# Seven-product units in attention's V, V ahead of Q in one head group, block moves over two queues

## The chip, the cores and the metric

The kernel runs on one core of one Trainium2 chip. The core's engines work side by side, each through its own queue in order: PE (TensorE: matmuls, with a weight load, PEld, ahead of each), DVE (VectorE), ACT (ScalarE), POOL (GpSimd) and SP (SyncE, here used only to start DMAs). DMAs are started by the queue of an engine and run beside the engines. The metric is the device time of one execution in microseconds, as a median over runs: 2028.35 us before (three runs, 2028.28 to 2033.81).

## The reference, cut to what matters

A decoder trunk of two layers on 256 tokens of 2048 channels. Layer 0 has a pooling mixer, layer 1 attention; each is followed by a gated feed-forward part and has two layer norms. The change is in layer 1's attention. Three dilated branches share q, k and v and are merged by their softmax denominators, which is one softmax over all keys, weighted by how many branches see a key:

```python
for i in range(DEPTH):                       # i = 1 is the attention layer
    ...
    k_shared = (h @ shared_w_k).reshape(B_, S, N_HEADS, HEAD_DIM)   # 16 heads of 128
    v_shared = (h @ shared_w_v).reshape(B_, S, N_HEADS, HEAD_DIM)
    mix = dilated_attention(h, k_shared, v_shared, attn_w_q[j], attn_w_o[j])
    h = layer_norm(DEEPNORM_ALPHA * h + mix, ln1_g[i], ln1_b[i])
...
def dilated_attention(h, k, v, w_q, w_o):
    q = (h @ w_q).reshape(B_, S, N_HEADS, HEAD_DIM)
    for window, dil in ((128, 1), (512, 4), (2048, 16)):
        o, lse = _dilated_branch(q, k, v, window, dil)
        ...
    o = jnp.sum(softmax(lses)[..., None] * outs, axis=0)
    return o.reshape(B_, S, D_MODEL) @ w_o
```

All is float32.

## The kernel before, in words

**Units.** Every weight matrix is read in blocks of 512 rows by 512 columns, one load of 1024 KB each on SP's queue. The list `units` holds one entry per block, in the order of the program; `run_units` walks it. For unit i it first calls `ahead(i)`: that issues the loads up to unit i+5 (three buffers `raw`) and the splits up to unit i+3 (four pairs of buffers `wh`, `wl`). A split makes two halves of a weight block whose sum is the weight: ACT casts the high half (L82), DVE subtracts it from the weight to get the low half (L83). x has been split in the same way. A product of float32 numbers is then two or three matmuls: high by high, low by high, high by low. After that come the matmuls of unit i. A function given to `later(n, fn)` runs after n further units; PE, DVE, ACT and SP get its instructions in their queues at that place.

**Three kinds of unit.** `group` (L165, L166) makes q, k and the output projection with the channels in the partitions: 16 matmuls of 512 columns and 16 of 256. `group_tm` (L238 to L240) makes v with the tokens in the partitions: 24 matmuls of 512 columns. The third kind, "seven products", is a form of a 2x2 block product (tokens in two halves, the block's columns in two halves, its rows in two halves) that takes seven block products instead of eight, at the price of sums of weights and sums of x. It is used in the feed-forward part before, not in attention. Its unit comes as two entries of the list with one load: part a (three products, 18 matmuls of 256 columns) and part b (four, 24 matmuls), L227 to L229. `split_sums` makes their weights: for a, two casts of ACT (L103), and on DVE a subtract (L104), two low halves (L106), two more subtracts (L107, L109); for b two casts (L96) and two low halves (L97). The seven leaves its results in four PSUM banks (`t0`, `t1`, `s2`, `s3`), and the function `early` has to add the last two banks in, five times a quarter.

**Attention.** Four head groups of four heads (hq 0 to 3). Before, each has four units of K, four of Q and four of V; sixteen units of the output projection follow. After the last unit of Q `qk_post` sets the rest: `scores` for heads 0 and 1, and one unit later for heads 2 and 3 (PE L988, L989, then a softmax, mostly on DVE, L994 to L1011); `blocks` turns the probabilities of two heads: a DVE transpose of 32x32 blocks (L1034) into the buffer `pb`, and then 16 DMAs that put the blocks in their places (L1043), of 32 partitions by six pieces of 32 numbers each, eight after one unit and eight after two, all on SP's queue. The buffer `pb` comes from the pool `hp` with five buffers, four of which hold the stream of layer 1, so one is free: the next block transpose waits until the DMAs of the one before have landed. `outputs` multiplies v by the turned probabilities (PE L1056, L1057) and splits the result (ACT, DVE L1059). For the last head group PE turns the probabilities itself (`transposes`, L1026), since there is little work between its softmax and the use.

Of the kernel before, what the change touches and what calls it, by code (L numbers as in the profile page):

```python
# [32 lines left out]
def trunk(ctx: ExitStack, tc: tile.TileContext, x, pool_w_in, pool_w_grp, pool_scale, pool_w_out,  # L33
# [14 lines left out]
    def bank(nm):  # L48
        return psp.tile([P, 512], F32, name=nm, tag="ps")
# [70 lines left out]
    def later(n, fn):  # L120
        if n == 0:
            fn()
        else:
            pending.append([n, fn])
# [157 lines left out]
    def quad_tile(nm):  # L282
        return xcp.tile([P, 4, 2, XW], F32R, name=nm, tag="xc")
# [659 lines left out]
    scale = 1.0 / math.sqrt(P)  # L943
    qk, pr, oq, pT, vts = {}, {}, {}, {}, {}

    def v_post(c):
        def post(t, ps):
            if t == 0:
                vts[c] = pools["attn"].tile([P, 2, 512], F32, name="vt", tag="vt")
                A.copy(vts[c][:, 0, :], ps)  # L950
            else:
                V.tensor_copy(vts[c][:, 1, :], ps)
                if c == 3:
                    later(1, lambda: transposes(c, (0, 1)))
                    later(2, lambda: transposes(c, (2, 3)))
                later(2 if c == 3 else 4, lambda: outputs(c, (0, 1)))
                later(3 if c == 3 else 7, lambda: outputs(c, (2, 3)))
        return post

    def qk_post(nm, hq):  # L960
        def post(ps):
            later(2 if hq == 0 and nm == "k" else 0, lambda: evac(ps))

        def evac(ps):
            ap = pools["attn"]
            o = ap.tile([P, 4, T], F32, name=nm, tag=nm)
            qk[nm] = o

            if hq == 0 and nm == "k":
                norm_evac(ps, 4, lambda m: o[:, m, :])  # L970
            else:
                for m in range(4):
                    A.copy(o[:, m, :], ps[m][:, T:])
                    V.tensor_tensor(o[:, m, :], o[:, m, :], ps[m][:, :T], OP.add)
            if nm == "q":
                later(2, lambda: scores(hq, range(0, 2)))
                later(3, lambda: scores(hq, range(2, 4)))
                if hq < 3:
                    later(4, lambda: blocks(hq, (0, 1)))
                    later(7, lambda: blocks(hq, (2, 3)))  # L980
        return post

    def scores(hq, ms):
        ap = pools["attn"]
        for m in ms:
            ps = bank("s")
            q, k = qk["q"][:, m, :], qk["k"][:, m, :]
            PE.matmul(ps[:, 0:P], q[:, :P], k[:, :P], start=True, stop=True)  # L988
# [24 lines left out]
    def turned(hq, ms):  # L1013
        pool, tag = (pools["attn"], "pT") if ms[0] == 0 else (lnp, "sq")
        t = pool.tile([P, 2, 3 * P], F32, name="pTs", tag=tag)
        for m in ms:
            pT[hq, m] = t[:, m % 2]
        return t

    def transposes(hq, ms):  # L1020
        t = turned(hq, ms)
        for m in ms:
            ps = bank("pT")
            s = pr.pop((hq, m))[0]
            for i in range(3):
                PE.transpose(ps[:, i * P:(i + 1) * P], s[:, i, :], ident)  # L1026
            A.copy(t[:, m % 2], ps[:, :3 * P])


    def blocks(hq, ms):  # L1030
        two = pr.pop((hq, ms[0]))[2]
        pr.pop((hq, ms[1]))
        b = hp.tile([P, 6 * P], F32, name="pb", tag="h")
        V.transpose(b, two.rearrange("p h s k -> p (h s k)"))  # L1034

        t = turned(hq, ms)
        to = t.rearrange("p h s -> p (h s)").rearrange("p (k a j) -> p a k j", k=6, a=4)
        fr = b.rearrange("p (k b j) -> p b k j", k=6, b=4)

        def move(rows):  # L1040
            for i in rows:
                for j in range(4):
                    nc.sync.dma_start(to[32 * j:32 * j + 32, i], fr[32 * i:32 * i + 32, j])  # L1043

        later(1, lambda: move((0, 1)))
        later(2, lambda: move((2, 3)))

    def outputs(hq, ms):
        if ms[0] == 0:
            oq[hq] = quad_tile("o")  # L1050
        vt = vts[hq]
        for m in ms:
            hd = slice(m * P, (m + 1) * P)
            ps = bank("o")
            t = pT.pop((hq, m))
# [12 lines left out]
    ffn(1)  # L1068
# [141 lines left out]
```

## Time and profile before

| | |
|---|---|
| median of three runs | 2028.35 us |
| profiled execution's own time | 2030.49 us |
| span of the profile | 2028.6 us |
| last matmuls of V: first, second, last head group | about 1000, 1073 and 1218 us of the span |
| granted PE clock over the span | full |

A row of instructions reads: start, duration, engine, line, operation, tiles out<-in, shapes, count; a bracket holds the idle time before it and what ended it. A row of the table of stretches gives, for each engine, busy time and (x) number of instructions, then the granted clock and the DMA share. A row of a wait reads: engine and operation that waits <- who ends it: total us, count, longest. "SPq" is SP's queue issuing DMAs. A row of issues gives the shortest/median/longest time (ns) of the issuing instruction, and a second line the time from issue to landing (us).

### The profile page before, as it was taken

The page shows a single profiled execution, that of the slowest core. Times are in us where ns is not written, and L with a number is a line of the kernel's source. Part 1 is how long each engine was busy: PE and PEld are TensorE (multiplying, and loading weights), DVE is VectorE, ACT ScalarE, POOL GpSimd, SP SyncE. Part 2 cuts the span into 40 slices and gives each one's busy share as a digit, 9 for nine tenths or more (in the row PEclk, how much of TensorE's full clock was granted, in tenths as well). Part 3 has the DMA queues.
Part 4 walks back from the last instruction along what each step waited for, and adds up shares of the span by engine and source line. Part 5 has one row for each costly group of instructions (what it writes and reads, how often), then busy time and mean ns, then how long its engine had stood idle before and what let it go on. Part 6 is the DMA issues. An engine that isn't in the chain of part 4 may idle for free.

```text
span 2028.6 us, 31127 instructions
## 1 busy us (share of the span) xinstructions
PE 2021.7 (100%) x12496; PEld 1809.4 (89%) x12496; DVE 1674.5 (83%) x1998; ACT 1257.2 (62%) x1685; POOL 75.0 (4%) x111
## 2 busy tenths in 40 slices
PE   9999999999999999999999999999999999999999
PEld 8898988899889988889888888998899989989987
DVE  6859887899789999879756657787889888989898
ACT  5544686667766676657533444577667676667672
POOL 2000000000000001100000000000000000100100
PEclk9999999999999999999999999999999999999999
DMA  8565467666655757864566554557666756666665
GB/s 257 201 206 188 165 209 210 190 192 225 210 191 187 234 188 219 232 226 165 191 197 195 169 185 168 187 178 216 187 198 197 228 187 213 198 213 196 209 214 180
DMA packets 278305, 405.92 MB, mean 200 GB/s; under 512 B 80414, under 2 KB 95668, under 8 KB 277904
## 3 DMA queue, kind: packets, MB, share of 16 engines
q1 hardware_dynamic: 266144, 389.72, 57.9%
q0 software_dynamic: 11584, 13.55, 4.4%
q8 instruction: 98, 1.61, 0.3%
q10 hardware_dynamic: 432, 0.66, 0.1%
q14 instruction: 47, 0.39, 0.1%
HBM read 380.01 MB, written 2.10 MB: 188 GB/s over the span
## 4 chain that ended last, share of the span: by engine, by line
PE 99%; DMA 0%; SPq 0%; DVE 0%; ACT 0%; issue 0%; DVEq 0%
PE acc L165 43%; PE acc L166 22%; PE t L238 3%; PE t L239 3%; PE t L240 3%; PE acc L169 3%; PE acc L170 3%; PE acc L168 3%; PE s L228 3%; PE s L229 3%; PE s L227 3%; PE t L228 2%; PE t L227 2%; PE t L229 2%; PE s L989 0%; PE o L1056 0%
## 5 line engine op out<-in xcount | busy, mean ns | idle before, releaser
L165 PE MATMUL acc<-xc,wh 128*128 128x512 f32 x3264 | 1151.9, 396 | 0.0
L166 PE MATMUL acc<-xc,wl 128*128 128x256 f32 x3264 | 916.3, 281 | 0.0
L83 DVE TENSOR_TENSOR wl<-raw,wh 128x2048 fp32r<-128x2048 f32 (+2 forms) x320 | 692.4, 2168 | 248.4 <-ACT wh L82 243.9
L165 PEld LDWEIGHTS acc<-xc,wh 128*128 128x128 f32 x3264 | 616.0, 189 | 143.7 <-DVE o L1059 0.6
L82 ACT CAST wh<-raw 128x2048 fp32r<-128x2048 f32 (+2 forms) x320 | 578.1, 1812 | 225.7 <-PE acc L165 118.3
L166 PEld LDWEIGHTS acc<-xc,wl 128*128 128x128 f32 x3264 | 615.5, 189 | 0.5
L96 ACT CAST wh<-raw 128x1024 fp32r<-128x1024 f32 x112 | 117.4, 1053 | 150.2 <-DVE raw L107 134.1
L97 DVE TENSOR_TENSOR wl<-raw,wh 128x1024 fp32r<-128x1024 f32 x112 | 133.8, 1221 | 0.5 <-ACT wh L96 0.5
L103 ACT CAST wh<-raw 128x1024 fp32r<-128x1024 f32 x112 | 87.7, 832 | 41.2 <-PE acc L165 24.7
L106 DVE TENSOR_TENSOR wl<-raw,wh 128x1024 fp32r<-128x1024 f32 x112 | 101.9, 951 | 1.3 <-ACT wh L103 0.9
L586 ACT ACTIVATE c<-u,cv 128x256 f32<-128x256 f32 x172 | 89.5, 593 | 19.4 <-DVE f L649 8.2
L228 PE MATMUL t<-wl,g 128*128 128x256 f32 x328 | 92.2, 281 | 0.0
L227 PE MATMUL t<-wh,g 128*128 128x256 f32 x328 | 92.1, 281 | 0.0
L229 PE MATMUL t<-wh,g 128*128 128x256 f32 x328 | 91.9, 280 | 0.0
L271 POOL DMA_DIRECT2D ht<-w x24 | 20.3, 847 | 1808.1 <-ACT wh L103 1060.1
L577 ACT COPY u<-acc 128x256 f32<-128x256 f32 x164 | 54.0, 372 | 46.9 <-PE acc L166 46.8
L229 PE MATMUL s<-wh,xs 128*128 128x256 f32 x296 | 82.6, 279 | 0.0
L228 PE MATMUL s<-wl,xs 128*128 128x256 f32 x296 | 82.6, 279 | 0.0
L227 PE MATMUL s<-wh,xs 128*128 128x256 f32 x296 | 82.5, 279 | 0.0
L591 ACT ACTIVATE a<-u,cv 128x256 f32<-128x256 f32 x172 | 73.6, 500 | 12.3 <-DVE g L659 6.5
L591 ACT ACTIVATE u<-u,cv 128x256 f32<-128x256 f32 x172 | 73.5, 500 | 0.0
L109 DVE TENSOR_TENSOR raw<-raw 128x1024 f32<-128x1024 f32 x56 | 68.6, 1225 | 1.9
(279 smaller groups left out, 3444.8 us busy)
## 6 DMA issues: line engine op xcount, KB each, us to landing
raw<-in_ffn_w_up_dram SPq DMA_DIRECT2D x160, 1024.0 KB, 4.9
raw<-in_ffn_w_down_dram SPq DMA_DIRECT2D x80, 1024.0 KB, 5.1
raw<-in_pool_w_out_dram SPq DMA_DIRECT2D x16, 1024.0 KB, 5.0
raw<-in_shared_w_k_dram SPq DMA_DIRECT2D x16, 1024.0 KB, 5.1
raw<-in_attn_w_q_dram SPq DMA_DIRECT2D x16, 1024.0 KB, 5.3
raw<-in_shared_w_v_dram SPq DMA_DIRECT2D x16, 1024.0 KB, 5.9
raw<-in_attn_w_o_dram SPq DMA_DIRECT2D x16, 1024.0 KB, 5.0
raw<-in_pool_w_in_dram SPq DMA_DIRECT2D x12, 1024.0 KB, 5.6
```

The source lines that it names most:

```text
L82: A.copy(wh[i][:, s], r[:, s])
L83: V.tensor_tensor(wl[i][:, s], r[:, s], wh[i][:, s].bitcast(F32), OP.subtract)
L96: A.copy(h[:, :, n], r[:, :, n])
L97: V.tensor_tensor(l[:, :, n], r[:, :, n], h[:, :, n].bitcast(F32), OP.subtract)
L106: V.tensor_tensor(l[:, k, n], r[:, k, n], h[:, k, n].bitcast(F32), OP.subtract)
L165: PE.matmul(ps[m], h[:, k, c], q[:, k, :, :T], start=st, stop=False)
L166: PE.matmul(ps[m][:, :T], l[:, k, c], q[:, k, 0, :T], start=False, stop=sp and not shifted)
L227: PE.matmul(to, xh, h[:, k, n], start=opens and kk == 0, stop=False)
L228: PE.matmul(to, xh, l[:, k, n], start=False, stop=False)
L229: PE.matmul(to, xl, h[:, k, n], start=False, stop=ends and kk == 1)
L586: A.activation(c[:, m, :], u[:, m, 2:], AF.Identity, scale=cv[:, 2, j:j + 1], bias=cv[:, 3, j:j + 1])
L591: A.activation(to[:, m, :], u[:, m, i:i + T], AF.Copy, scale=cv[:, i, j:j + 1])
```

## The change

In the second, third and fourth head group some of the four V units become sevens: three in the second group (its units 1, 2, 3), three in the third, one in the fourth (unit 3). The sums of x that they need are formed once, in `v_sums`, on DVE and ACT, for the three quarters of x used, one after another at the end of the units that follow the first group's Q; a seven's v is added together by `v_early` and `v_post`. In the second head group V stands between K and Q. The block moves of a batch are issued together, eight on SP's queue and eight on POOL's. The last head group uses block transposes and moves too, and PE's transposes are gone. The distances in units after Q at which scores, block transposes and outputs come are written out for each group.

```diff
     def v_post(c):
         def post(t, ps):
-            if t == 0:
-                vts[c] = pools["attn"].tile([P, 2, 512], F32, name="vt", tag="vt")
-                A.copy(vts[c][:, 0, :], ps)
+            v = v_tile(c)[t]
+            if c > 0:
+                V.tensor_tensor(v, v, ps, OP.add)
+            elif t == 0:
+                A.copy(v, ps)
             else:
-                V.tensor_copy(vts[c][:, 1, :], ps)
-                if c == 3:
-                    later(1, lambda: transposes(c, (0, 1)))
-                    later(2, lambda: transposes(c, (2, 3)))
-                later(2 if c == 3 else 4, lambda: outputs(c, (0, 1)))
-                later(3 if c == 3 else 7, lambda: outputs(c, (2, 3)))
+                V.tensor_copy(v, ps)
         return post
 
+    def v_early(c):
+        def early(p16, p75):
+            v0, v1 = v_tile(c)
+            left, right = v0[:, :256], v0[:, 256:]
+            A.copy(left, p16[:, :256])
+            V.tensor_tensor(right, left, p16[:, 256:], OP.add)
+            V.tensor_tensor(v1[:, :256], right, p75[:, :256], OP.add)
+            V.tensor_tensor(right, right, p75[:, 256:], OP.add)
+            V.tensor_tensor(v1[:, 256:], v1[:, :256], p75[:, 256:], OP.add)
+        return early
+
+    vsums = {}
+
+    def v_sums(q, then):
+        ap = pools["attn"]
+        x = H[q]
+        a11, a12, a21, a22 = (x[:, k:k + 2, t * P:t * P + P] for k, t in ((0, 0), (2, 0), (0, 1), (2, 1)))
+        f = ap.tile([P, 4, T], F32, name="f", tag="k")
+        d = [f[:, i].rearrange("p (k t) -> p k t", k=2) for i in range(4)]
+        V.tensor_tensor(d[0], a21, a22, OP.add)
+        V.tensor_tensor(d[1], d[0], a11, OP.subtract)
+        V.tensor_tensor(d[2], a21, a11, OP.subtract)
+        V.tensor_tensor(d[3], a12, d[1], OP.subtract)
+
+        def rest():
+            if q < 3:
+                t = quad_tile("xsum")
+                vsums[q] = [[t[:, i, hl, :T].rearrange("p (k t) -> p k t", k=2) for hl in range(2)] for i in range(4)]
+                split_act(t, f)
+                then()
+                return
...
+        later(1, rest)
...
             if nm == "q":
-                later(2, lambda: scores(hq, range(0, 2)))
-                later(3, lambda: scores(hq, range(2, 4)))
-                if hq < 3:
-                    later(4, lambda: blocks(hq, (0, 1)))
-                    later(7, lambda: blocks(hq, (2, 3)))
+                s0, b0, b1, o0, o1 = ((2, 4, 7, 8, 11), (2, 4, 7, 12, 14), (9, 11, 14, 15, 18), (2, 3, 5, 7, 8))[hq]
+                later(s0, lambda: scores(hq, range(0, 2)))
+                later(b0, lambda: blocks(hq, (0, 1)))
+                later(s0 + 1, lambda: scores(hq, range(2, 4)))
+                later(b1, lambda: blocks(hq, (2, 3)))
+                later(o0, lambda: outputs(hq, (0, 1)))
+                later(o1, lambda: outputs(hq, (2, 3)))
+                if hq == 0:
+                    later(4, lambda: v_sums(3, lambda: v_sums(1, lambda: v_sums(2, lambda: None))))
         return post
...
-        def move(rows):
-            for i in rows:
+        def move():
+            for i in range(4):
                 for j in range(4):
-                    nc.sync.dma_start(to[32 * j:32 * j + 32, i], fr[32 * i:32 * i + 32, j])
-
-        later(1, lambda: move((0, 1)))
-        later(2, lambda: move((2, 3)))
+                    by = nc.sync if i < 2 else nc.gpsimd
+                    by.dma_start(to[32 * j:32 * j + 32, i], fr[32 * i:32 * i + 32, j])
+
+        later(1, move)
...
+    def v_group(hq):
+        js = (0, 1, 2, 3)
+        seven = {0: (), 1: (1, 2, 3), 2: (1, 2, 3), 3: (3,)}[hq]
+        group_tm(shared_w_v, rows4, 512 * hq, 512, xsrcs, v_post(hq),
+                 seven={j: (lambda j=j: vsums[j]) for j in js if j in seven}, early=v_early(hq))
+
     for hq in range(4):
         x0 = hq == 0
         group(shared_w_k, rows4, 512 * hq, 512, psrcs if x0 else xsrcs, qk_post("k", hq), mode="x" if x0 else "ab")
+        if hq == 1:
+            v_group(hq)
         group(attn_w_q[0], rows4, 512 * hq, 512, xsrcs, qk_post("q", hq))
-        group_tm(shared_w_v, rows4, 512 * hq, 512, xsrcs, v_post(hq))
+        if hq != 1:
+            v_group(hq)
```

PE's queue after the second head group's K, where the first group's first two outputs are made, reads as follows before the change (`wh210` is the high half of the 211th unit's weights, `xc` the split x, `acc` a bank of q).

```order
L1056 MATMUL o_9938<-pTs_9758,vt_9759 128x256
L1057 MATMUL o_9938<-pTs_9758,vt_9759 128x128
L1056 MATMUL o_9943<-pTs_9758,vt_9759 128x256
L1057 MATMUL o_9943<-pTs_9758,vt_9759 128x128
L165 MATMUL acc_9971<-xc_9247,wh210_9814 128x512
L166 MATMUL acc_9971<-xc_9247,wl210_9815 128x256
```

After the change, at the end of the first V unit, which follows the same outputs, and the start of the first seven (`t0`, `t1`, `s2` are banks of v):

```order
L238 MATMUL t1_10023<-wh210_9844,xc_9247 128x512
L239 MATMUL t1_10023<-wl210_9845,xc_9247 128x512
L240 MATMUL t1_10023<-wh210_9844,xc_9247 128x512
L227 MATMUL s2_10024<-wh211_9890,xc_9310 128x256
L228 MATMUL s2_10024<-wl211_9891,xc_9310 128x256
L229 MATMUL s2_10024<-wh211_9890,xc_9310 128x256
```

V's plain unit and its sevens have come to where Q's first unit stood.

SP's queue around the first of the second head group's two batches before (`raw` is a buffer of a weight block, the number behind x counts the DMAs of a row):

```order
L72 DMA raw_10302<-in_attn_w_q_dram 128x4x512
L72 DMA raw_10338<-in_attn_w_q_dram 128x4x512
L1043 DMA pTs<-pb 32x6x32 x8
L72 DMA raw_10388<-in_attn_w_q_dram 128x4x512
L1043 DMA pTs<-pb 32x6x32 x8
L72 DMA raw_10434<-in_attn_w_q_dram 128x4x512
```

The moves of both of the second head group's batches stand on SP after the change like this:

```order
L72 DMA raw_10582<-in_shared_w_v_dram 128x4x512
L72 DMA raw_10632<-in_shared_w_v_dram 128x4x512
L1081 DMA pTs<-pb 32x6x32 x8
L72 DMA raw_10726<-in_shared_w_v_dram 128x4x512
L1081 DMA pTs<-pb 32x6x32 x8
L72 DMA raw_10835<-in_shared_w_v_dram 128x4x512
```

A batch now has one row of eight on SP instead of two, with a load between them; the other eight stand on POOL's queue, 64 in all, one row behind another.

DVE's queue at the end of the last head group after the change (`pb` the turned blocks, `vt` v, `wl250` the low half of an output projection's unit):

```order
L1062 TENSOR_SCALAR p_11659<-p_11659,mx_11671 128x256
L83 TENSOR_TENSOR wl250_11690<-raw250_11550,wh250_11689 128x2048
L83 TENSOR_TENSOR wl251_11730<-raw251_11613,wh251_11729 128x2048
L1068 STREAM_TRANSPOSE pb_11757<-p_11659 128x768
L967 TENSOR_TENSOR vt_11760<-vt_11760,s2_11524 128x256
L968 TENSOR_TENSOR vt_11760<-vt_11760,s3_11525 128x256
L969 TENSOR_TENSOR vt_11760<-vt_11760,s3_11525 128x256
L970 TENSOR_TENSOR vt_11760<-vt_11760,s3_11525 128x256
L955 TENSOR_TENSOR vt_11760<-vt_11760,t0_11522 128x512
L955 TENSOR_TENSOR vt_11760<-vt_11760,t1_11523 128x512
L83 TENSOR_TENSOR wl252_11771<-raw252_11687,wh252_11770 128x2048
L1096 TENSOR_TENSOR o_11864<-o_11865,o_11864 128x256
```

Before, the same place held one copy of v and the splits:

```order
L1011 TENSOR_SCALAR p_11426<-p_11426,mx_11438 128x256
L83 TENSOR_TENSOR wl244_11457<-raw244_11332,wh244_11456 128x2048
L952 COPY vt_11484<-t1_11307 128x512
L83 TENSOR_TENSOR wl245_11490<-raw245_11393,wh245_11489 128x2048
L83 TENSOR_TENSOR wl246_11543<-raw246_11454,wh246_11542 128x2048
L1059 TENSOR_TENSOR o_11589<-o_11590,o_11589 128x256
```

The block transpose has come in ahead of the six adds that make v, and those ahead of the next split.

More of the change, by code (lines that the diff above doesn't have):

```diff
@@ L944, in trunk, with v_tile @@
     qk, pr, oq, pT, vts = {}, {}, {}, {}, {}
+    def v_tile(c):
+        if c not in vts:
+            vts[c] = pools["attn"].tile([P, 2, 512], F32, name="vt", tag="vt")
+        return vts[c][:, 0, :], vts[c][:, 1, :]
     def v_post(c):
         def post(t, ps):
-            if t == 0:
-                vts[c] = pools["attn"].tile([P, 2, 512], F32, name="vt", tag="vt")
-                A.copy(vts[c][:, 0, :], ps)
-            else:
-                V.tensor_copy(vts[c][:, 1, :], ps)
-                if c == 3:
-                    later(1, lambda: transposes(c, (0, 1)))
-                    later(2, lambda: transposes(c, (2, 3)))
-                later(2 if c == 3 else 4, lambda: outputs(c, (0, 1)))
-                later(3 if c == 3 else 7, lambda: outputs(c, (2, 3)))
@@ new lines, in trunk @@
+    vsums = {}
[16 more added lines that the diff above has]
+                return
+            w = lnp.tile([P, 2, T], F32R, name="vs0", tag="fold2")
+            z = ap.tile([P, 2, T], F32R, name="vs3", tag="vs3")
+            vs = [[w[:, 0], w[:, 1]], [z[:, 0], z[:, 1]]]
+            for pair in (("S", "Q"), ("cs", "f1")):
+                vs.append([lnp.tile([P, T], F32R, name=f"vs{nm}", tag=nm) for nm in pair])
+            for i, v in enumerate(vs):
+                A.copy(v[0], f[:, i])
+            for i, v in enumerate(vs):
+                V.tensor_tensor(v[1], f[:, i], v[0].bitcast(F32), OP.subtract)
+            vsums[q] = [[u.rearrange("p (k t) -> p k t", k=2) for u in v] for v in vs]
+            then()
+        later(1, rest)
@@ L1011, in scores @@
                 V.tensor_scalar(sf[:, sl], sf[:, sl], mx[:, t:t + 1], None, op0=OP.mult)
[L1013 to L1027, printed above, removed]
     def blocks(hq, ms):
@@ L1034, in blocks @@
         V.transpose(b, two.rearrange("p h s k -> p (h s k)"))
-        t = turned(hq, ms)
+        pool, tag = (pools["attn"], "pT") if ms[0] == 0 else (lnp, "sq")
+        t = pool.tile([P, 2, 3 * P], F32, name="pTs", tag=tag)
+        for m in ms:
+            pT[hq, m] = t[:, m % 2]
         to = t.rearrange("p h s -> p (h s)").rearrange("p (k a j) -> p a k j", k=6, a=4)
         fr = b.rearrange("p (k b j) -> p b k j", k=6, b=4)
-        def move(rows):
-            for i in rows:
+        def move():
+            for i in range(4):
                 for j in range(4):
-                    nc.sync.dma_start(to[32 * j:32 * j + 32, i], fr[32 * i:32 * i + 32, j])
-        later(1, lambda: move((0, 1)))
-        later(2, lambda: move((2, 3)))
+                    by = nc.sync if i < 2 else nc.gpsimd
+                    by.dma_start(to[32 * j:32 * j + 32, i], fr[32 * i:32 * i + 32, j])
+        later(1, move)
     def outputs(hq, ms):
```

## The prediction

> **What bounds the kernel now.** The first views are the head of the profile's page and its chain of waits.
>
> ```profile
> span 2028.6 us, 31127 instructions
> PE 2021.7 (100%) x12496; PEld 1809.4 (89%) x12496; DVE 1674.5 (83%) x1998; ACT 1257.2 (62%) x1685; POOL 75.0 (4%) x111
> ...
> PE 99%; DMA 0%; SPq 0%; DVE 0%; ACT 0%; issue 0%; DVEq 0%
> ```
>
> PE is the whole chain, so a matmul left out is time won, and any wait that reaches PE is time lost. The second view is the table of stretches, over attention and over two units of v's kind.
>
> ```profile
> core 0: us, PE busy (x) PEld busy (x) DVE busy (x) ACT busy (x) POOL busy (x), PEclk, DMA share, GB/s
> 964.00:1243.00 279.00, 279.00 (x1474) 238.37 (x1473) 175.04 (x286) 120.55 (x140) 0.00 (x0) 1.00 0.58 186
> 1047.86:1059.00 11.14, 11.14 (x50) 9.03 (x49) 5.04 (x4) 4.09 (x3) 0.00 (x0) 1.00 0.55 191
> 1509.47:1514.46 4.99, 4.99 (x45) 4.99 (x44) 4.92 (x6) 2.56 (x3) 0.00 (x0) 1.00 0.60 208
> ```
>
> In attention PE has no gap, DVE is busy 63% (175.04 of 279.00), POOL does nothing, and the granted clock is full: no slower clock is there to be won back. The third row is two plain v units (48 matmuls of 512 columns), the fourth one unit in seven products in the feed-forward part (42 of 256). Their ends in the timeline:
>
> ```profile
> 1047.86 0.40 PE L238 MATMUL t<-wh,xc 128*128 128x512 f32 x1
> ...
> 1058.78 0.40 PE L240 MATMUL t<-wh,xc 128*128 128x512 f32 x1
> 1509.47 0.28 PE L227 MATMUL s<-wh,g 128*128 128x256 f32 x1
> ...
> 1514.34 0.28 PE L229 MATMUL s<-wh,xs 128*128 128x256 f32 x1
> ```
>
> **The gain: sevens and transposes.** A plain unit takes 11.14/2 = 5.57 us, a seven 4.99, so each of the seven saves 0.58: 4.1 us. In the last head group two batches of PE transposes go, both on the chain:
>
> ```profile
> 1224.12 0.66 PE pT L1026 x6
> ...
> 1230.40 0.66 PE pT L1026 x6
> ```
>
> That is 1.3 more, 5.4 us in all if nothing waits. It is 0.27%; about 0.3%, 6.1 us, is what a measurement of this kernel can tell from no change.
>
> **DVE's extra work.** In the seven's stretch PEld is busy throughout and DVE 4.92 of 4.99. Its rows:
>
> ```profile
> 1510.21 0.69 DVE L104 TENSOR_TENSOR raw<-raw 128x512 f32<-128x512 f32 x1
> 1510.81 1.82 DVE L106 TENSOR_TENSOR wl<-raw,wh 128x1024 fp32r<-128x1024 f32 x2
> 1512.67 0.69 DVE L107 TENSOR_TENSOR raw<-raw 128x512 f32<-128x512 f32 x1
> 1513.39 1.23 DVE L109 TENSOR_TENSOR raw<-raw 128x1024 f32<-128x1024 f32 x1
> 1514.56 2.41 DVE L97 TENSOR_TENSOR wl<-raw,wh 128x1024 fp32r<-128x1024 f32 x2
> 1013.31 2.29 DVE L83 TENSOR_TENSOR wl<-raw,wh 128x2048 fp32r<-128x2048 f32 x1 [3.32 <-ACT wh L82]
> ```
>
> A seven takes 6.8 us of DVE (0.69 + 1.82 + 0.69 + 1.23 + 2.41), a plain unit 2.29. Three sevens in a row need 20.5 of DVE against 15 us of PE. The lead of three units covers that in the third head group, where little else stands on DVE. In the second, the rest of v's sums and the first group's softmax stand ahead. With each instruction laid end to end, the last half of the third seven is ready some 1.2 us before PE wants it, so I take 0. PE has no gap there now that a split could close, so the lower end is 0 too; the upper is 3 us, half a seven's DVE time late. The sums of x are 12 operations of 256 columns, which cost 0.42 each by
>
> ```profile
> L645 DVE TENSOR_TENSOR f<-c 128x256 f32<-128x256 f32 x17 | 7.1, 418 | 0.0
> ```
>
> that is 5 us, and 4.3 with lower parts (three further subtracts of 1024 columns), spread over four ends of units. They delay the first head group's second block transpose by some 4 us, used below. v's sums afterwards are adds of DVE straight from PSUM. V ahead of Q in the second group moves no work off PE: price 0, since q and k there are used five units later or more.
>
> **The block moves: the price that decides.** Before, SP issues all 16 DMAs of a batch; now SP eight, and POOL eight.
>
> ```profile
> 1003.37 6.00 SPq L1043 DMA_DIRECT2D pTs<-pb  x8
> ...
> 1018.06 6.67 SPq L1043 DMA_DIRECT2D pTs<-pb  x8
> ```
>
> SP's eight take 6 us or so. No row shows POOL issuing such a DMA, which moves 32 partitions of six pieces of 128 bytes, 192 pieces. The nearest rows:
>
> ```profile
> 399.82 0.92 POOL L271 DMA_DIRECT2D ht<-w  x1 [316.24 <-ACT wh L103]
> 400.43 2.06 POOL L271 DMA_DIRECT2D ht<-u  x2
> ...
> 30.91 1.89 POOL L1122 DMA_DIRECT2D crow<-in_ffn_conv_w_dram  x1
> ```
>
> Three DMAs of 128 rows end 2.66 us after the first began (400.43 + 2.06 − 399.82 = 2.67), 0.89 each, 6.9 ns a row: 1.33 for 192. The convolution weights are 86 × 3 = 258 pieces in 1.89, 7.3 ns each: 1.40. I take t = 1.36 per DMA, as both neighbours agree on it; the ends are 0.61 (400.43 − 399.82, if only the pitch of two starts counted) and 1.89 (the larger row as it stands). Eight cost 8t = 10.9 us, later than SP's by 5. The data land after the issue ends:
>
> ```profile
> L271 POOL DMA_DIRECT2D ht<-w x24: 832/842/915, 399.8 to 1951.5; - x24
> DMA to landing us min/median/max: 3.3/4.8/7.6
> L1117 POOL DMA_DIRECT2D vrow<-in_ln_g_dram x4: 484/504/672, 28.3 to 34.3; - x4
> DMA to landing us min/median/max: 1.7/2.0/8.8
> ```
>
> 3.3 − 0.84 = 2.5 and 1.7 − 0.5 = 1.2; I take 2.0. The Trainium skill ("DMA: Bandwidth & Descriptors", section "Issuing engines are not separate DMA queues") says that spreading DMAs over issuers saves only the cost of issuing; by that, the split gains nothing once the second issuer is the slower one, as POOL is by the rows above.
>
> What it delays is the second block transpose: its target buffer is the only spare one, so it waits until all of the first batch has landed, and DVE's queue stands behind it. That wait exists already:
>
> ```profile
> DVE pb L1034 <- DMA pTs<-pb: 4.4, 3, 2.3
> 1017.02 0.98 DVE L1034 STREAM_TRANSPOSE pb<-p 128x768 f32<-128x768 f32 x1 [1.42 <-DMA pTs<-pb]
> ```
>
> *Last head group.* Counted from the end of v's third unit (zero). Scores, then softmax:
>
> ```profile
> 1204.55 0.38 PE L988 MATMUL s<-k,q 128*128 128x128 f32 x2
> ...
> 1210.79 2.29 DVE L83 TENSOR_TENSOR wl<-raw,wh 128x2048 fp32r<-128x2048 f32 x1
> ```
>
> A pair of heads takes 6.25 us from scores to the end of softmax. The first pair's scores stand at −6.9, so softmax ends at −0.6; a split (to 1.65) and o's lower parts (2.3) come next, and the transpose ends at 3.3. POOL then issues until 3.35 + 10.9 = 14.2; landed 16.2. Meanwhile DVE does the second pair's softmax and two splits, to 13.3, so it stands still for 3 us. The second transpose ends at 17.2, POOL's second batch at 28.2, landed 30.2. PE, from the first outputs and scores (2.6, two pairs at 1.3, by the gap between the units around an output in
>
> ```profile
> 1040.77 0.28 PE L166 MATMUL acc<-xc,wl 128*128 128x256 f32 x1
> ...
> 1042.43 0.28 PE L166 MATMUL acc<-xc,wl 128*128 128x256 f32 x1
> ```
>
> 1.66 less a plain step's 0.36), goes through the seven (4.76, 7.6) and two units of the output projection (13.2, 18.9), then wants the first pair of outputs; v's sums (3.2 us of DVE after the second transpose) are ready at 20.4, 1.5 late. It wants the second pair at 25.8 plus those 1.5; the blocks come at 30.2. PE stands 4.4 us in all. With t up to 1.09 it stands not at all; above that each 0.1 of t costs 1.6.
>
> *First head group.* With v's sums on DVE the second transpose ends at 1022.1 (before: 1018.0), POOL at 1033.0, landed 1035.0; PE wants it at 1034.5, the end of the first seven of the second group's v: 0.5. It is free up to t = 1.29. The two groups between have 4 us or more to spare.
>
> Sum: −5.4 + 4.4 + 0.5 = −0.5. The profiled execution, 2030.49, becomes 2030.0; the median, 2028.35, stands 2.1 below it, and the sum moved there gives 2027.8, say 2028.
>
> **Rivals.**
> - B, *all hidden*: POOL takes 1.1 or less per DMA. For it: 16 rows take 0.50 (the layer norm's vectors) and 128 rows 0.89, a line that gives 1.11 at 192. Against: on that line 258 would take 1.34, and the row shows 1.89. Time: 2028.35 − 5.4 = 2023.
> - C, *slower by POOL's issue*: t = 1.89, the row of the weights as it stands, if pieces are not what counts but strided forms. Then the last group stands 12.8 us and the first 4.8: +12, 2040.5. It is slower by over 6.1 from t = 1.64 on (24t − 33.2 = 6.1). Against it: 1.33 and 1.40, by count of pieces, agree within 0.07.
> - D, *splits late*: the second group's three sevens starve PE of the last halves, up to 3 us: 2031. For it the 20.5 against 15 us; against it the lead of three units.
> - E, *POOL writes its DMAs only while DVE rests*. DVE rests 39% of a stretch with v:
>
> ```profile
> 1036.00:1109.00 73.00, 73.00 (x387) 62.37 (x387) 44.41 (x71) 30.20 (x34) 0.00 (x0) 1.00 0.58 184
> 1533.12 2.35 DVE L97 TENSOR_TENSOR wl<-raw,wh 128x1024 fp32r<-128x1024 f32 x2
> 1533.13 0.84 POOL L271 DMA_DIRECT2D ht<-w  x1 [36.09 <-DVE ht L853]
> 1533.67 2.05 POOL L271 DMA_DIRECT2D ht<-u  x2
> ```
>
> 44.41 of 73.00 is busy, so t = 1.36/0.39 = 3.5, and 24t − 33.2 is 51 more: above 2079. Against it: the three DMAs that ran beside the two subtracts from 1533.12 took 2.59 (1533.67 + 2.05 − 1533.13), no more than the 2.67 elsewhere. The Trainium skill ("SBUF — State Buffer", section "SBUF: two separate sides") warns of it: POOL cannot write descriptors while a DVE operation of a two-port mode holds the port they share; from its 620 ns alone and some 3100 beside such an operation (5 times), an estimate of t is 6.8, and 24t − 33.2 is 130. The trace does not agree for these subtracts.
>
> **How the numbers follow.** The forecast 0.42 (t between 1.1 and 1.6), B 0.31, C 0.17, D 0.07, E 0.03. The forecast lies within 0.3%, and so does most of B, 0.7 us inside the bound, but for 0.08 in which it gains a little more; D lies within up to 3 us. Faster 0.08, same 0.67, slower 0.25 (C, E, and 0.05 of D and of the forecast where t and late splits add up). The range runs from just past B, 2022, to 2037 (t about 1.75), which leaves E and the upper half of C out, and a few hundredths below. The forecast's own range is 2023.5 to 2034.
>
> **What would show it.** Right: a seven's pitch in v near 4.99 us, no transposes of PE, POOL's block DMAs near 1.36 each and eight in 10.9, a DVE wait of some 3 us at the last group's second transpose, and PE gaps only ahead of the last group's outputs, some 4 us together. Wrong: POOL rows under 1.1 with no gaps (B), rows of 1.9 (C), idle PEld in the second group's sevens after a subtract of L97 (D), rows that stretch where DVE is busy (E).

## The result and the profile after

The changed kernel takes 2023.72 us (median of 8 runs, 2023.22 to 2024.69) against 2029.09 for the kernel before (8 runs): 5.4 us less, a ratio of 0.997 with a 95% interval of 0.9959 to 0.9981. The interval leaves out 1, though the prediction had put the least difference that can be told at 0.3%. Executions of one kernel spread by 2 us and more: the profiled one of before, 2030.49, was granted a clock of 0.66 from 10 to 15 us of its span, the profiled one of the changed kernel, 2024.13, a clock of 1.00, and that alone is an estimated 1.7 us ((1 − 0.66) × 5). Lowest against lowest, the change gives 5.0. The time lies in the range, and it is the rival B, "all hidden" (2023), that came true, not the forecast of 2028: the gain was sized rightly, and the stalls that were to eat it did not come.

The head of the page and its chain of waits, after:

```profile
span 2022.0 us, 31645 instructions
PE 2014.2 (100%) x12610; PEld 1809.2 (89%) x12610; DVE 1719.5 (85%) x2075; ACT 1270.1 (63%) x1708; POOL 111.3 (6%) x175
...
PE 99%; DMA 0%; SPq 0%; DVE 0%; ACT 0%; issue 0%; DVEq 0%
```

PE is still the whole chain, with 114 more matmuls (each of the seven sevens has 18 more than a plain unit, of half the columns, and 12 transposes are gone). DVE has 45 us more work and POOL 36, and neither shows on the chain. The table of stretches after: K, Q and V with the first outputs; one plain unit of V; two sevens in a row in the second head group; the last group, from the third group's last outputs to its own last ones.

```profile
core 0: us, PE busy (x) PEld busy (x) DVE busy (x) ACT busy (x) POOL busy (x), PEclk, DMA share, GB/s
962.00:1236.50 274.50, 274.50 (x1596) 241.57 (x1595) 220.75 (x364) 134.15 (x164) 36.23 (x64) 1.00 0.63 192
1022.80:1028.48 5.68, 5.68 (x27) 4.60 (x26) 5.41 (x12) 2.94 (x8) 2.52 (x5) 1.00 0.75 153
1034.69:1044.72 10.03, 10.03 (x87) 10.03 (x86) 9.96 (x10) 6.53 (x7) 0.00 (x0) 1.00 0.42 147
1205.10:1232.32 27.22, 27.22 (x172) 24.67 (x171) 23.93 (x41) 12.88 (x15) 9.03 (x16) 1.00 0.77 212
```

PE has no gap in any of them, the last group included, and the clock is full. A seven takes 10.03/2 = 5.01 us, as forecast (4.99), though DVE is busy 9.96 of 10.03 there. What PE's weight loads waited for between 1000 and 1270 us, the only row:

```profile
PEld acc L165 <- DVE o L1096: 0.2, 1, 0.2
```

The price of the block moves, by the queue that issued them (shortest/median/longest, ns):

```profile
L1081 SPq DMA_DIRECT2D pTs<-pb x64: 585/604/1290, 1002.3 to 1225.0; - x64
L1081 POOL DMA_DIRECT2D pTs<-pb x64: 572/572/630, 1003.0 to 1224.3; - x64
```

And the last head group's two transposes and two batches in the timelines of DVE and POOL:

```profile
1208.14 0.98 DVE L1068 STREAM_TRANSPOSE pb<-p 128x768 f32<-128x768 f32 x1 [0.71 <-DVE o L1096]
...
1218.85 0.97 DVE L1068 STREAM_TRANSPOSE pb<-p 128x768 f32<-128x768 f32 x1
```

```profile
1209.69 4.51 POOL L1081 DMA_DIRECT2D pTs<-pb  x8 [24.92 <-issue]
1220.39 4.52 POOL L1081 DMA_DIRECT2D pTs<-pb  x8 [6.18 <-issue]
```

POOL takes 0.57 us for a move, less than SP's 0.60, where 1.36 had been forecast; eight take 4.5 us. The second transpose waits for nothing: the first batch has landed by 1216.2, and DVE comes to the transpose at 1218.85. The second batch has landed at 1228.6; PE comes to it at 1230.9.

### The profile page after: what moved, and what is told of

Read it like the earlier page. It is cut to its first block, busy times and chain, and to the rows that moved or that the text cites. A ratio compares the mean times of both kernels' runs of the same rounds, so it can differ in the third digit from the quotient of the medians.

```text
span 2022.0 us, 31645 instructions
## 1 busy us (share of the span) xinstructions
PE 2014.2 (100%) x12610; PEld 1809.2 (89%) x12610; DVE 1719.5 (85%) x2075; ACT 1270.1 (63%) x1708; POOL 111.3 (6%) x175
## 4 chain that ended last, share of the span: by engine, by line
PE 99%; DMA 0%; SPq 0%; DVE 0%; ACT 0%; issue 0%; DVEq 0%
PE acc L165 44%; PE acc L166 22%; PE s L228 3%; PE s L227 3%; PE s L229 3%; PE acc L169 3%; PE acc L170 3%; PE acc L168 3%; PE t L238 3%; PE t L240 3%; PE t L239 3%; PE t L228 2%; PE t L227 2%; PE t L229 2%; PE s L1040 0%; PE o L1093 0%
## 5 line engine op out<-in xcount | busy, mean ns | idle before, releaser
L83 DVE TENSOR_TENSOR wl<-raw,wh 128x2048 fp32r<-128x2048 f32 (+2 forms) x313 | 676.0, 2165 | 207.8 <-ACT wh L82 206.4
L82 ACT CAST wh<-raw 128x2048 fp32r<-128x2048 f32 (+2 forms) x313 | 564.8, 1810 | 201.7 <-PE acc L165 92.2
L96 ACT CAST wh<-raw 128x1024 fp32r<-128x1024 f32 x126 | 131.7, 1053 | 170.9 <-DVE raw L107 135.5
L97 DVE TENSOR_TENSOR wl<-raw,wh 128x1024 fp32r<-128x1024 f32 x126 | 150.4, 1221 | 3.5 <-ACT wh L96 3.5
L103 ACT CAST wh<-raw 128x1024 fp32r<-128x1024 f32 x126 | 98.7, 834 | 47.8 <-PE acc L165 24.6
L106 DVE TENSOR_TENSOR wl<-raw,wh 128x1024 fp32r<-128x1024 f32 x126 | 114.7, 951 | 4.2 <-ACT wh L103 4.0
L109 DVE TENSOR_TENSOR raw<-raw 128x1024 f32<-128x1024 f32 x63 | 77.2, 1225 | 2.1
```

The source lines that it names most:

```text
L82: A.copy(wh[i][:, s], r[:, s])
L83: V.tensor_tensor(wl[i][:, s], r[:, s], wh[i][:, s].bitcast(F32), OP.subtract)
L96: A.copy(h[:, :, n], r[:, :, n])
L97: V.tensor_tensor(l[:, :, n], r[:, :, n], h[:, :, n].bitcast(F32), OP.subtract)
L103: A.copy(h[:, k, n], r[:, k, n])
L106: V.tensor_tensor(l[:, k, n], r[:, k, n], h[:, k, n].bitcast(F32), OP.subtract)
```

## The experiments

Times of experiments are compared with the changed kernel's 2023.72; the ratios are to the kernel before, run beside them.

**The price of a DMA on POOL by itself.** A kernel of its own:

```diff
+    for j in range(4):
+        G.dma_start(six(a)[32 * j:32 * j + 32, 1], fr[0:32, j])
...
+    for j in range(4):
+        G.dma_start(b[:, j].rearrange("p (k j) -> p k j", k=6), fr[:, j])
...
+        G.dma_start(c[:, j], src[:, 256 * j:256 * j + 256])
...
+        G.dma_start(d[:, j], src[:, 256 * j:256 * j + 256], accum_op=OP.add)
...
+        G.dma_start(e[:, j], ffn_conv_w[j % 2].rearrange("j (k p) -> k j p", p=P))
...
```

> Computes nothing of the trunk (its output is x): DMAs on POOL's queue alone, four of each form: 32x6x32 (192 pieces, the block move), 128x6x32 (768 pieces), 128x256 plain and with accumulation, the convolution weights' form 86x3x128 and a form 80x3x128, the biases' 86x128; then eight block moves each beside subtracts and beside copies of DVE. Theory (POOL's price is nearly fixed per DMA, and accumulation and the form of 86 rows by 3 are what made the two rows dear from which the forecast took its price): 0.5 to 0.65 for 32x6x32, 128x6x32, 128x256 plain, 86x128 and 80x3x128; 0.85 with accumulation; 1.9 for 86x3x128. Rival 1 (the forecast's: by count of pieces): 128x256 plain 0.89 like the accumulating one, 128x6x32 over 2, 80x3x128 1.7. Rival 2 (POOL waits where DVE holds a shared port): 0.57 beside subtracts, and rows of 1.5 us or more beside copies.

POOL's timeline of this kernel, with the first of DVE's copies (DMAs of one form stand in one row: start, time from the first one's start to the last one's end; the last row repeats the two last DMAs of the row ahead of it):

```profile
18.72 2.37 POOL L36 DMA_DIRECT2D blk<-src  x4 [18.27 <-DVE src L27]
21.08 3.32 POOL L39 DMA_DIRECT2D wide<-src  x4
24.39 2.16 POOL L42 DMA_DIRECT2D plain<-src  x4
26.54 3.55 POOL L46 DMA_DIRECT2D acc<-src  x4
28.73 8.71 POOL L49 DMA_DIRECT2D conv<-in_ffn_conv_w_dram  x4
36.10 3.45 POOL L52 DMA_DIRECT2D conv<-in_ffn_conv_b_dram  x4
...
43.64 0.64 POOL L55 DMA_DIRECT2D eighty<-in_ffn_conv_w_dram  x1 [1.05 <-DMA conv<-in_ffn_conv_b_dram]
46.99 4.64 POOL L69 DMA_DIRECT2D msub<-ssub  x8 [2.71 <-DVE ssub L63]
63.62 8.41 POOL L69 DMA_DIRECT2D mcpy<-scpy  x8 [11.99 <-DVE scpy L65]
63.24 7.53 DVE L72 COPY three<-two 128x2048 f32<-128x2048 f32 x6
70.89 1.14 POOL L69 DMA_DIRECT2D mcpy<-scpy  x2
```

A move of 192 pieces takes 2.37/4 = 0.59, one of 768 pieces 0.83: 576 more pieces for 0.24 us, 0.4 ns each, not 7. A plain DMA of 128 rows takes 0.54. From the accumulating form on, a row begins before the row ahead of it has ended, so a price is read from end to end. With accumulation it is 0.89 (26.54 + 3.55 = 30.09, less 26.55, by four), though these four begin only 0.55 apart, like the plain ones. The form of 86 rows by three takes 1.84 (37.44 − 30.09, by four), 86 rows of one piece 0.53, 80 rows of three 0.64. So the forecast's first row was dear by its accumulation, and its second by the form of 86 rows by three; neither the 86 rows alone (0.53) nor the count (240 pieces for 0.64) makes it dear, and no run shows what does. The theory holds, but for the 768 pieces, which it had at 0.65 at most, and the count of pieces falls as a measure.

Of rival 2 the direction holds, not the size. Beside subtracts of DVE a move takes 4.64/8 = 0.58. Beside copies the first six take (70.89 − 63.62)/6 = 1.21 each, about as long as one copy (7.53/6 = 1.25); the copies end at 70.77, and the two moves behind them take 0.57 again. The Trainium skill ("SBUF — State Buffer", section "SBUF: two separate sides") gives float32 copies within SBUF as a case that locks POOL out while it writes descriptors, at 5 times the price. These rows agree in kind, at 2.1 times. The attention part has no copies within SBUF beside its moves (its one copy of DVE there reads a PSUM bank).

**POOL made as slow as forecast.** POOL clears a scratch tile four times behind each of its moves (the kernel `pool_135` has three); the lines that make the tile are left out here:

```diff
...
                     by.dma_start(to[32 * j:32 * j + 32, i], fr[32 * i:32 * i + 32, j])
+                    for _ in range(4 if i >= 2 else 0):
+                        nc.gpsimd.memset(scrap[0], 0.0)
```

> Behind each of POOL's 64 block moves POOL clears a scratch tile of 128 x 128 four times (0.2 us each), with no DMA and no wait, so that a move holds POOL for 0.57 + 0.8 = 1.37 to 1.4 us: the price that the forecast took. Theory (the forecast's reckoning of what waits was right, its price was not): PE gaps of 4 to 5 us in all ahead of the last group's outputs and 0.5 to 1 us ahead of the first group's second outputs. By the forecast's sum 2028 to 2029; with the lower granted clock that stood for 2.5 to 4 us behind each gap of 4 to 7 us in the two kernels before, 1.5 to 2 us more per gap: 2029 to 2032. Rival (at that price the moves are hidden): 2024, no gap.

2044.20, ratio 1.0068 (1.0054 to 1.0082): above both. PE stood 15.2 us in three gaps. A part is that a clearing took longer than planned; POOL's timeline in the last group:

```profile
1237.46 0.57 POOL L1084 DMA_DIRECT2D pTs<-pb  x1
1238.01 1.01 POOL L1086 MEMSET scrap<- 128x128 f32 x4
1239.06 0.57 POOL L1084 DMA_DIRECT2D pTs<-pb  x1
```

1239.06 − 1237.46 = 1.60 per move. With three clearings:

> As the kernel with four clearings behind each of POOL's block moves, where a move held POOL for 1.60 us, but with three, so that it holds POOL for about 1.34: the price that the forecast took (1.36). Theory (the price was wrong, and beside it the time from the end of a batch's issue to its landing, which was taken as 2.0 and was 3.8 to 5.0 in the last group and 4.5 in the first group's second batch at 1.60; and a gap costs 1.7 more by the lower clock behind it): gaps of 2.5 ahead of the first group's second outputs and of 8 ahead of the last group's, 10 to 11 in all and up to 5 by the clock: 2036 to 2039. Rival (the forecast's sum holds at its own price): 4.9 us of gaps, 2028 to 2030.

2037.77, ratio 1.0044 (1.0030 to 1.0057), in the theory's band and 8 us above the rival's. Here a move holds POOL for 1.34 us. From 1.34 to 1.60 the time rises by 6.4 us, 25 for each us of t, the slower clock behind the gaps included; the forecast's formula has 24. PE's waits between 1000 and 1270 us, the wait of DVE's transposes, and the landing of the moves from 1205 to 1245 us (from the start of an issue):

```profile
PE o L1098 <- DMA pTs<-pb: 4.1, 1, 4.1
PE o L1098 <- DVE vt L956: 3.1, 1, 3.1
PE o L1098 <- DVE wl L106: 0.8, 1, 0.8
```

```profile
DVE pb L1069 <- DMA pTs<-pb: 7.6, 2, 4.9
```

```profile
DMA to landing us min/median/max: 1.7/2.3/5.6
```

The waits stand where the forecast put them: v late for the first pair of the last group's outputs (3.1), the second batch late for the second pair (4.1), and 0.8 at the first group's second outputs (put down to a split that had long been done; the batch landed there at 1035.2, and PE went on at 1035.8). But they come to 8.0 where its formula gives 4.4 at t = 1.34. What it had too short is the landing: the forecast let the last block land 2.0 us after the end of its issue; in the last group it took 4.1 and 4.6. These 4.7 us more cover the missing 3.6, so other terms of the ledger must have been somewhat too long. That the clearings slowed DVE instead does not show: two splits take 4.49 us in this trace and in that of the changed kernel. So at the forecast's own price the change would have been slower than before, by 8 to 9 us.

Of the 14.1 us over the changed kernel, 8.0 are gaps of PE and an estimated 3.4 the half clock behind two of them (last section). The rest has no row that shows it.

**POOL slowed by small DMAs.** Two DMAs of 32 numbers behind each move instead of the clearings (the lines that make `scrap` are left out here):

```diff
...
                     by.dma_start(to[32 * j:32 * j + 32, i], fr[32 * i:32 * i + 32, j])
+                    for _ in range(2 if i >= 2 else 0):
+                        c = scrap[1]
+                        by.dma_start(scrap[0][:, c:c + 1], ident[0:32, 0:1])
+                        scrap[1] += 1
```

> Behind each of POOL's 64 block moves POOL issues two small DMAs (32 rows of one number) into a scratch tile, so that a move holds POOL for about 0.57 + 2 x 0.49 = 1.55 us. Theory (the forecast's reckoning of the waits was right and only its price per move was wrong): by 24t - 33.2 with t = 1.55, 4 us over the time before: about 2033, with a wait of DVE at the last group's second block transpose, a PE gap of 7 to 10 us ahead of the last group's outputs and one of 2 us ahead of the first group's second outputs. Rival (the moves are hidden also at that price): 2024, no PE gap.

2049.85, ratio 1.0100 (1.0086 to 1.0114), 17 us above the theory, with 19.3 us of gaps in PE, so this run does not tell the price of a wait. POOL itself waited for earlier DMAs to land:

```profile
1010.12 0.50 POOL L1088 DMA_DIRECT2D scrap<-ident  x1 [0.89 <-DMA pTs<-pb]
...
1015.82 0.99 POOL L1088 DMA_DIRECT2D scrap<-ident  x2 [1.49 <-DMA scrap<-ident]
```

**All moves on SP.**

```diff
-                    by = nc.sync if i < 2 else nc.gpsimd
+                    by = nc.sync
```

> All 16 block moves of a batch on SP's queue; all else as in the changed kernel. Theory (POOL issues a move as fast as SP, 0.57 us against 0.60, so the split halves the issue of a batch and nothing stands in the last head group): 16 moves take 10 us instead of 5. In the last head group the first batch is then issued from 1209.2 to 1219.2 and landed at about 1221, the second transpose ends at 1222 instead of 1219.8, the second batch is issued until 1232 and landed at about 1235, while PE wants it at 1230.9: PE waits about 4 us there, and nowhere else; about 2028 us. Rival 1 (the loads of the output projection, now behind 16 moves on SP, come late too): PE also waits ahead of a unit of the output projection, 2029 to 2032. Rival 2 (the split over two queues was worth nothing): 2024.

2032.53, ratio 1.0018 (1.0009 to 1.0027): the split is worth 8.8 us, twice what the theory gave. SP's queue in the last group, the waits of weight loads and of DVE, and the two stretches at and behind the gap:

```profile
1209.75 11.17 SPq L1081 DMA_DIRECT2D pTs<-pb  x16
1223.38 12.05 SPq L1081 DMA_DIRECT2D pTs<-pb  x16
```

```profile
PEld o L1093 <- issue: 5.0, 2, 4.5
PEld s L228 <- DVE wl L97: 1.5, 1, 1.5
...
DVE raw L104 <- DMA raw<-in_shared_w_v_dram: 5.7, 2, 4.2
```

```profile
1233.00:1237.10 4.10, 0.00 (x0) 0.00 (x0) 0.95 (x1) 0.00 (x0) 0.00 (x0) 0.96 0.27 46
1237.10:1240.00 2.90, 2.85 (x9) 2.52 (x10) 0.43 (x1) 0.37 (x1) 0.00 (x0) 0.50 0.99 359
```

The gap ahead of the last outputs is the 4 us expected (4.2 on PE, 4.5 for the weight load). Two things came on top. Behind the gap the granted clock is 0.50 for 3 us. And the weights of V stood behind 16 moves on SP: DVE waited 4.2 us for them, where it waits 1.2 in the changed kernel, so a seven's split was late and PE's weight load waited 1.5 us in the second head group, which the expectation had denied. The margin of the three sevens in a row is that thin. Rival 1's wait ahead of a unit of the output projection does not show. The Trainium skill ("DMA: Bandwidth & Descriptors", section "Issuing engines are not separate DMA queues") says, as the prediction cited it, that more issuers save only the cost of issuing. This run agrees, but here that cost decided: without the second queue the change is slower than the kernel before. The prediction's own case, a slower second queue, is the kernel with three clearings, and there the split was worse than none: 2037.8 against 2032.5.

**The sevens alone undone.**

```diff
...
-                s0, b0, b1, o0, o1 = ((2, 4, 7, 8, 11), (2, 4, 7, 12, 14), (9, 11, 14, 15, 18), (2, 3, 5, 7, 8))[hq]
+                s0, b0, b1, o0, o1 = ((2, 4, 7, 8, 10), (2, 4, 7, 10, 11), (6, 8, 11, 12, 15), (2, 3, 4, 6, 7))[hq]
...
-                if hq == 0:
-                    later(4, lambda: v_sums(3, lambda: v_sums(1, lambda: v_sums(2, lambda: None))))
...
-        seven = {0: (), 1: (1, 2, 3), 2: (1, 2, 3), 3: (3,)}[hq]
+        seven = ()
```

> All of v's units plain, the sums of x left out, and scores, transposes and outputs at the same places of the program; the moves over two queues, V ahead of Q and the last group's block transposes stay. Theory: 7 x (5.57 - 4.99) = 4.1 us more than the changed kernel, 2027.8. Rival 1 (the sevens also lost something to late splits, or won more by what stands next to them): 3 us or 5 us more instead. Rival 2 (the gain came from the queues and the order, not from the sevens): within 1 us of 2023.7.

2027.49, ratio 0.9989 (0.9981 to 0.9998): 3.8 us more than with them. The theory's 4.1 fits, and rival 2 falls. By the times alone rival 1's 3 or 5 us are not excluded, since the interval is 3.4 us wide; the traces speak against them, as PE waits for nothing in this part in either kernel, and seven times the difference of the pitches, 5.57 − 5.01, is 3.9.

**The last group's transposes back on PE.**

```diff
-                s0, b0, b1, o0, o1 = ((2, 4, 7, 8, 11), (2, 4, 7, 12, 14), (9, 11, 14, 15, 18), (2, 3, 5, 7, 8))[hq]
+                s0, b0, b1, o0, o1 = ((2, 4, 7, 8, 11), (2, 4, 7, 12, 14), (9, 11, 14, 15, 18), (2, 6, 7, 7, 8))[hq]
...
-                later(b0, lambda: blocks(hq, (0, 1)))
+                later(b0, lambda: (blocks if hq < 3 else transposes)(hq, (0, 1)))
...
-                later(b1, lambda: blocks(hq, (2, 3)))
+                later(b1, lambda: (blocks if hq < 3 else transposes)(hq, (2, 3)))
...
```

> The last head group turned by PE transposes again, as before the change, one and two units after V; all else as in the changed kernel. Theory: 12 transposes on the chain, 2 x 0.66 = 1.3 us more: 2025.0, no PE gap in either. Rival (the last group's block moves held something up that is free with PE's transposes): the same time or less, 2023 to 2024.

2024.92, ratio 0.9977 (0.9968 to 0.9986): 1.2 us more, as the theory has it. By its size it is within what the runs scatter, so it supports the theory without excluding the rival.

**V behind Q in the second group.**

```diff
-                s0, b0, b1, o0, o1 = ((2, 4, 7, 8, 11), (2, 4, 7, 12, 14), (9, 11, 14, 15, 18), (2, 3, 5, 7, 8))[hq]
+                s0, b0, b1, o0, o1 = ((2, 4, 7, 8, 11), (9, 11, 14, 19, 21), (9, 11, 14, 15, 18), (2, 3, 5, 7, 8))[hq]
...
-        if hq == 1:
-            v_group(hq)
         group(attn_w_q[0], rows4, 512 * hq, 512, xsrcs, qk_post("q", hq))
-        if hq != 1:
-            v_group(hq)
+        v_group(hq)
```

> V behind Q in the second head group too, scores, transposes and outputs of that group at the same places of the program; all else as in the changed kernel. Theory (the order moves no work off PE): the same within 1 us, 2023.7. Rival (V ahead of Q keeps the three sevens' splits clear of the first group's and the second group's softmax): PE waits for a split in the second group's sevens, 1 to 4 us more.

2023.51, ratio 0.9971 (0.9960 to 0.9982): the same. With the uses at the same places the order is worth nothing here.

**One more seven.**

```diff
-                s0, b0, b1, o0, o1 = ((2, 4, 7, 8, 11), (2, 4, 7, 12, 14), (9, 11, 14, 15, 18), (2, 3, 5, 7, 8))[hq]
+                s0, b0, b1, o0, o1 = ((2, 4, 7, 8, 11), (2, 4, 7, 12, 14), (9, 11, 14, 16, 18), (2, 4, 6, 8, 9))[hq]
...
-        seven = {0: (), 1: (1, 2, 3), 2: (1, 2, 3), 3: (3,)}[hq]
+        seven = {0: (), 1: (1, 2, 3), 2: (1, 2, 3), 3: (2, 3)}[hq]
```

> One more seven in the last head group (units 2 and 3 instead of 3 alone), places of the last two groups shifted by the one entry more. Theory (DVE has room there, a seven is worth what it was elsewhere): 0.6 us less, 2023.1, no new gap. Rival (the last group's DVE is full, with softmax, adds and splits): a gap ahead of a unit or of the last outputs, 2024 to 2027.

2027.35, ratio 0.9991 (0.9983 to 1.0000): 3.6 us more, the rival's time. PE's weight loads waited; with them the stretches around the two gaps, and DVE's second transpose of the last group:

```profile
PEld o L1093 <- issue: 2.2, 1, 2.2
PEld acc L166 <- DVE wl L83: 2.1, 1, 2.1
```

```profile
1213.67:1217.00 3.33, 1.07 (x6) 0.55 (x5) 3.29 (x5) 3.33 (x3) 0.00 (x0) 1.00 0.00 0
1227.70:1231.50 3.80, 1.90 (x11) 1.30 (x10) 3.66 (x7) 2.27 (x2) 3.35 (x6) 1.00 1.15 307
```

```profile
1226.60 0.98 DVE L1068 STREAM_TRANSPOSE pb<-p 128x768 f32<-128x768 f32 x1 [4.67 <-DMA pTs<-pb]
```

The first unit of the output projection waits for its split: DVE is full there (3.29 of 3.33), and so is ACT. The last group's outputs wait for another reason: v's adds stand on DVE behind the second transpose, and DVE stood still for 4.7 us ahead of it until the first batch had landed. The two gaps of PE, 2.3 and 1.9 us, less the 0.6 that the seven saves, make the 3.6. With these places of the transposes the last group bears one seven.

## Why the prediction was right in the time and wrong in its reason

- *The gain, 5.4 us in all: right.* The sevens are worth 3.8 (forecast 4.1) and the transposes 1.2 (1.3), by undoing each, though the second is within the runs' scatter; the whole change gave 5.4, and 5.0 lowest against lowest.
- *DVE's extra work, 0: right.* The ledger gave the last half of the third seven 1.2 us of margin; in the trace its first low half is ready at 1040.1 and PE uses it at 1042.0, 1.9 us. With all moves on SP the load came 3.0 us later, and that used it up. One more seven in the last group cost 3.6, by the split and the transpose there.
- *V ahead of Q, 0: right.*
- *The price of a move on POOL, t = 1.36: wrong*, 0.57 measured. This is the step that failed. It scaled two rows by their count of pieces, and each had another reason to be dear: one accumulates, the other has the form of 86 rows by three. That the two agreed within 0.07 was chance. The lower end that it named and put aside, 0.61 from start to start of the accumulating DMAs, came nearest. A row of the trace before spoke against the count, and the prediction did not use it:

```profile
32.78 0.57 POOL L1123 DMA_DIRECT2D crow<-in_ffn_conv_b_dram  x1
```

  86 pieces in 0.57, beside the 16 in 0.50 that rival B quoted: 0.001 us per piece, and 192 would have been 0.68. With it the forecast would have been B's, since by its ledger the stalls begin at t = 1.09.
- *The landing, 2.0 us after the issue: wrong too*, up to 5 us in the runs at 1.34 and 1.60. In the changed kernel it takes 1.25 in the last group's first batch, 3.0 in its second, where 2.2 us are left before PE would wait, and 5.4 in the first group's second. From the start of an issue to the landing the median is 3.9 us with two queues and 1.9 with all moves on SP; what lengthens it no run isolates. At the forecast's price the kernel took 2037.8, beyond the range's end of 2037: the range held by luck, because the larger error pointed the other way.
- *Where the stalls would stand* was right: with POOL slowed, PE waits in the last group ahead of both pairs of outputs and DVE waits 4.9 us at the second transpose, as the forecast had it at 3. One term that it had too long: the first group's second transpose, 4 us later by the ledger, ends at 1019.6 after the change against 1018.0 before, 1.6 later.
- *Rival E* is seen beside DVE's copies, not beside the subtracts that stand there. The rows of subtracts that the prediction set against it could not speak for copies.

## What to carry to other kernels

A price that is scaled by one property of a row (pieces, bytes) needs a second row that differs in that property alone; take every row of the same engine and operation, the cheap ones too, before choosing. Where records of one queue overlap, read a price from end to end or from start to start, and say which. When a batch's landing releases the next step, reckon the landing by the longest of the distribution, since the last DMA of the batch decides. And what a second issuing queue is worth shows in what stands behind the batch: here a gap of 4.2 us, the slower clock behind it, and a late load.

## What the prediction had not expected of the hardware

After a gap of some microseconds PE does not go on at full speed. The stretches behind the gaps, in the kernel with three clearings and, in the last row, in the one with two small DMAs (the column ahead of the last two is the granted clock):

```profile
1229.79:1233.20 3.41, 3.41 (x11) 2.89 (x12) 3.41 (x3) 1.12 (x3) 3.00 (x12) 0.50 0.40 57
1233.21:1238.10 4.89, 4.89 (x29) 4.26 (x28) 4.20 (x4) 1.42 (x1) 4.37 (x15) 1.00 0.91 279
1242.57:1243.44 0.87, 0.87 (x5) 0.82 (x6) 0.00 (x0) 0.00 (x0) 0.00 (x0) 1.00 0.86 315
1243.45:1246.85 3.40, 3.40 (x13) 2.84 (x12) 0.85 (x2) 2.54 (x3) 0.00 (x0) 0.50 0.03 11
1239.70:1243.50 3.80, 3.72 (x11) 3.23 (x12) 3.80 (x3) 1.15 (x3) 3.80 (x8) 0.50 0.38 51
```

Behind gaps of 3.1, 4.1 and 5.7 us the granted clock was 0.50 for 3.4 to 3.7 us of work, in one case only from 0.9 us after PE went on; behind the shorter gaps, of 0.8 us here and of up to 2.3 with one more seven, it stayed 1.00. What that costs is seen with all moves on SP, from the second matmul of the output projection to the first but one of its fifth unit, there (first row; in the second the part of it behind the gap) and in the changed kernel (third row):

```profile
1214.35:1245.98 31.63, 27.20 (x146) 23.16 (x145) 20.27 (x23) 11.74 (x12) 0.00 (x0) 0.95 0.61 188
1237.15:1240.22 3.07, 3.07 (x9) 2.67 (x10) 0.43 (x1) 0.51 (x2) 0.00 (x0) 0.50 1.00 367
1213.03:1238.25 25.22, 25.22 (x146) 22.03 (x145) 21.17 (x29) 12.51 (x12) 5.70 (x11) 1.00 0.82 233
```

31.63 us against 25.22 for the same 146 matmuls: 6.4 more. Of these, 4.4 are gaps, and PE was busy 2.0 longer; 3.07 us at half the clock account for some 1.5 of that. A stall of PE of this length thus costs a third to a half more than its length; the prediction had priced stalls at their length alone. The Trainium skill ("TensorE: Matmul & The Clock Gate", section "Part 1: The HAM clock gate (the "warmup" mystery)") states that an idle window of about 3.4 us halves PE's clock, and that about 3.4 us of activity restore it. The rows agree with the half and with the length, though a gap of 3.1 us was already enough. By the page, 3.4 us at half speed lose an estimated 1.7 us, where 1.5 to 2.0 are seen.
